# When the second half's tokens get their adaLN modulation: at the change of halves on ScalarE, or tile by tile ahead of it on VectorE

## The chip, the cores and the metric

The kernel runs on one core of one Trainium2 chip. The metric is the device time of one execution in microseconds. TensorE multiplies matrices; VectorE (DVE), ScalarE (ACT) and GpSimd (POOL) work on tiles in the on-chip memory; SyncE (SP) only issues transfers. The engines run on their own and wait for each other by semaphores.

## The reference

One layer of a decoder trunk over 2048 prompt tokens of width 1024, and 8 sample tokens. What matters here is how every projection's input comes about:

```python
ada = jax.nn.silu(c) @ w_ada + b_ada
shift, scale, gate = jnp.split(ada, 3, axis=-1)
hn = _rmsnorm(x, g_norm) * (1.0 + scale[:, None]) + shift[:, None]
z = hn @ w_in
xa, za, q, k, v, glr, zg = jnp.split(z, SPLITS, axis=-1)
# xa, za: conv, block-diagonal gates and a linear recurrence, gated by silu(za)
# q, k, v, glr, zg: 4 heads of gated linear attention, gated by silu(zg)
mix = jnp.concatenate([y_lru, y_gla], axis=-1) @ w_out
x = x + gate[:, None] * mix
```

The two groups' results go through one output projection, and a last RMSNorm follows. `scale` and `shift` are one number for each of the 1024 channels.

## The kernel before

The prompt is computed in two halves of 1024 tokens, first all projections, recurrence and attention of half 0, then those of half 1. For a half, `hn` lies transposed in SBUF, channels on the partitions: `hh` holds its values rounded to TensorE's 32-bit format and `hl` what the rounding left. Every projection is three matmuls for each slice of 128 channels, `acc<-hh,w`, `acc<-hl,w`, `acc<-hh,w` (L679 to L681; L364 to L366 for the values of the attention). Results are evicted from four accumulators, by ScalarE and VectorE: `vh` and `vl` (L975, L976) for values, `zs` (L1148, L1149) for gated columns.

Half 1's `hn` is prepared beside half 0's work. `turn_ahead(q)`, for q = 0 to 7, handles 128 tokens: SP loads `x` (L248); ScalarE squares it and sums (L166); VectorE makes the reciprocal root in twelve tiny operations (`rsqrt`, L148 to L154), scales the tile (`times`, L182) and transposes it in blocks of 32x32 (L253); SP stores it to DRAM (`xtd`, L257). The steps are put into a list by `after(units, fn)`, which counts units of TensorE's work, and are issued when their time has come: so their place in each engine's queue is fixed when the program is built, and an engine that comes to a step whose input is missing waits there with all that stands behind it.

At the change of halves `lru_last_a` projects the first group's last column block of half 0 and meanwhile fills `hh` and `hl` anew, in four groups g of 256 tokens. `hn_load` gathers the stored blocks (20 loads; twelve of them, `xst<-xtd` L277, stand together on SP). `modulate` takes scale (`Gm`) and shift (`Sh`) per channel on ScalarE (L201; a part of g = 3 on VectorE, L203) into `fs4` and `ra`, GpSimd rounds to `hh` (L204, 16 times), VectorE subtracts for `hl` (L205, 16 times). TensorE runs four gate projections of 256 tokens each there (`silu2`, evicted by `zs`). The steps of `modulate` are drawn one by one from the list `drips`. Behind them `sums` (L1508, L1512, L1517 on VectorE, L1511 on ScalarE) adds and subtracts the parts in `fs4` and `ra` to the operands `so` of seven products that stand for eight (L1576).

Other names in the prediction: `on` is an attention output chunk, normalized by L1108 and transposed by TensorE in L1182; `e`, `xb` and `g` belong to the decay of the attention (`decay` and `gla_decay`, L996 to L1045; TensorE takes `xb` in L1060); `tx`, `tg` and the scan (L1349 to L1353) are the recurrence; `cv`, `xh`, `xl` the conv and its rounding; `tr`, `th` prepare weights of pairs; `w<-wr` and `parts` prepare weights.

Of the kernel before, what the change touches and what calls it, by code (L numbers as in the profile page):

```python
# [54 lines left out]
def hybrid_kernel(ctx, tc, i, o):  # L55
    nc = tc.nc
    V, S, G, PE, SP = nc.vector, nc.scalar, nc.gpsimd, nc.tensor, nc.sync
# [117 lines left out]
    def scales(pool, ss, n, m=P):  # L175
        rs = pool.tile([P, 4], F32, tag="rs", name="rs", bufs=2)
        rsqrt(pool, rs[:m, :n], ss[:m, :n], n, m, 1.0 / D)
        return rs

    def times(xt, rs, m=P, j0=0):  # L180
        for j, x in enumerate(xt, j0):
            V.tensor_scalar(x[:m], x[:m], rs[:m, j:j + 1], None, op0=OP.mult)  # L182
# [2 lines left out]

        times(xt, scales(pool, squares(pool, xt, m, tag), len(xt), m), m)

    def modulate(xt, g, kts):

        c = slice(g * 256, (g + 1) * 256)  # L190
        pt = [x.rearrange("p (n k t) -> p k n t", k=KT, t=32) for x in xt]
        for k2 in range(kts[0], kts[1], 2):
            cg = slice(g % 2 * 256, g % 2 * 256 + 256)
            f = (fs4[(1, 2, 0)[k2 // 4 if g < 2 else 2]][:, k2 % 4:k2 % 4 + 2, cg] if g < 2 or k2 >= 4
                 else ra[k2 // 2][:, :, cg])
            for kt in range(k2, k2 + 2):
                for j, y in enumerate(pt):
                    n = 256 // len(pt)
                    z = f[:, kt - k2, j * n:(j + 1) * n].rearrange("p (n t) -> p n t", t=32)
                    if g < 3 or kt == k2:  # L200
                        S.activation(z, y[:, kt], AF.Identity, scale=Gm[:, kt, 8:9], bias=Sh[:, kt, 8:9])  # L201
                    else:
                        V.tensor_scalar(z, y[:, kt], Gm[:, kt, 8:9], Sh[:, kt, 8:9], op0=OP.mult, op1=OP.add)  # L203
            G.tensor_scalar(hh[:, k2:k2 + 2, c], f, 1.0, 0.0, op0=OP.mult, op1=OP.add)  # L204
            V.tensor_tensor(hl[:, k2:k2 + 2, c], f, hh[:, k2:k2 + 2, c].bitcast(F32), op=OP.subtract)  # L205

    def turn(xt, k):

# [36 lines left out]
    def turn_ahead(q):  # L245

        x, w = [xp.tile([P, TH + NS], F32, tag="xt", name="xt")[:, :D] for _ in range(2)]
        SP.dma_start(x, i["x_prompt"][0, TH + q * P:TH + (q + 1) * P])  # L248

        def scaled(ss):  # L250
            with behind(V):
                times([x], scales(xp, ss, 1))
                V.transpose(w.rearrange("p (c k j) -> p c k j", c=4, k=KT), x.rearrange("p (k c j) -> p c k j", c=4, k=KT))  # L253
# [7 lines left out]
        def squared():  # L261
            ss = squares(xp, [x])
            after(0.5, lambda: scaled(ss))

        after(2, squared)

    def hn_load(g):

        if g == 0:
            xt = [xp.tile([P, TH + NS], F32, tag="xt", name="xt")[:, :D] for _ in range(2)]  # L270
        else:
            xt = [xst[g - 1].rearrange("p q d -> p (q d)")]
        m = 2 // len(xt)
        for j, x in enumerate(xt):
            src = xtd[2 * g + j * m:2 * g + j * m + m].rearrange("q (a r) (c f) -> c r (q a) f", a=4, c=4)
            for c in range(4):
                SP.dma_start(x[32 * c:32 * c + 32].rearrange("r (n f) -> r n f", f=256), src[c])  # L277
        return xt

    fs = cp.tile([P, KT, NS], F32, name="fs")  # L280

# [457 lines left out]
    def ada_gate():  # L739

        pg = acc()

        def step(kt):
            ws = [xp.tile([P, TH + NS], F32, tag="xt", name="xt")[:, :D] for _ in range(2)]
            for n, w in enumerate(ws):
                SP.dma_start(w, i["w_ada"][0, (kt + n) * P:(kt + n + 1) * P, 2 * D:])

            def mm():
                for n in (1, 0):
                    for g in range(4):  # L750
# [12 lines left out]
        step(0)  # L763


    so, fs4, xst, ra, waiting = {}, [], [], [], ["gate", "pairs"]
    outw = {"stop": False, "next": None, "busy": False}

    def ready(what):
# [674 lines left out]
            for s in range(len(t.segs)):  # L1444
                za_unit(t, s)

    def next_hn(xt, g, k):

        modulate(xt[g], g, (k, k + 4))

    def lru_last_a(js):

        xa_load, xa_unit, za_load, za_unit = lru_units(0)
        xt = [hn_load(0)]
        lru(0, js[:-2])
        outw["stop"] = True
        lru(0, js[-2:-1])
        t = xa_load(js[-1])
        za_load(t)
        flush_gla()  # L1460
        while outw["busy"]:
            heapq.heappop(pend)[2]()
        open_sp()
        xt += [hn_load(1), hn_load(2), hn_load(3)]
        for s in range(2):
            xa_unit(t, s)
            za_unit(t, s)
            for g in range(2 * s, 2 * s + 2):
                for k in range(0, KT, 4):
                    drips.extend([lambda g=g, k=k: next_hn(xt, g, k), lambda: None])  # L1470

    spx = ExitStack()
    sp_ = None
# [1 line left out]
    def open_sp():  # L1475
        gpx.close()
        hpx.close()
        nonlocal sp_
        sp_ = spx.enter_context(tc.tile_pool(name="sp", bufs=1, side="right", reuse_waits="tile"))
        fs4[:] = [sp_.tile([P, 4, 512], F32, tag=f"s{n}", name="fs4") for n in range(2)]  # L1480
        xst[:] = [sp_.tile([P, 2, D], F32, tag=f"s{n}", name="xst") for n in range(3, 6)]
        fs4.append(sp_.tile([P, 4, 512], F32, tag="s2", name="fs4"))
        ra[:] = [new_ra(F32) for _ in range(2)]

# [17 lines left out]

    def sums():

        s1, s2, s4 = fs4

        def sub(x, y, z):
            V.tensor_tensor(x, y, z, op=OP.subtract)  # L1508

        def split(h, l, x):  # L1510
            S.copy(h, x)  # L1511
            V.tensor_tensor(l, x, h.bitcast(F32), op=OP.subtract)  # L1512

        def step(n, u):
            k = slice(2 * u, 2 * u + 2)
            if n == 0:
                V.tensor_tensor(s1[:, k], s1[:, k], ra[u], op=OP.add)  # L1517
                sub(ra[u], s2[:, k], ra[u])
                sub(s2[:, k], s1[:, k], s2[:, k])
            elif n == 3:  # L1520
                h, l = a21()
                split(h[:, k], l[:, k], ra[u])
            elif n == 4:
                if u == 0:
                    so[ZB22] = new_so(1), [new_ra(F32R) for _ in range(2)]
                h, l = so[ZB22]
                split(h[:, k], l[u], s4[:, k])
            else:
                if u == 0:
                    so[(ZT1, ZT2)[n - 1]] = [new_so(j) for j in ((3, 4), (5, 0))[n - 1]]  # L1530
                if n == 2:
                    sub(s4[:, k], s4[:, k], s2[:, k])
                h, l = so[(ZT1, ZT2)[n - 1]]
                split(h[:, k], l[:, k], (s1, s2)[n - 1][:, k])
# [741 lines left out]
```

## Time and profile before

| | us |
|---|---|
| median of 3 runs | 1459.3 (1457.58 to 1460.83) |
| the profiled execution | 1459.87 |
| its span | 1458.1 |
| TensorE busy in it | 1420.3 |
| VectorE, ScalarE, GpSimd busy | 1062.8, 692.9, 220.8 |

The mean granted clock is 0.992. In the timelines, a row gives start and duration in us, the engine, the line, the operation with output and inputs, the tile's shape, how many followed each other, and in brackets the idle time ahead of it and what ended it. Operations overlap a little on an engine, so the distance from start to start is shorter than the duration.

### The profile page before, as it was taken

What the parts mean: (1) busy time and instruction counts of PE and PEld (TensorE: products, weight loads), DVE (VectorE), ACT (ScalarE), POOL (GpSimd) and SP (SyncE); (2) the same over time, 40 slices, a digit from 0 to 9 for tenths busy, and PEclk for the clock granted to TensorE, in tenths of its full rate; (3) what the DMA queues carried; (4) which work ended last, traced back from release to release, by engine and by line L of the source; (5) the groups of instructions that cost most, each with busy time, mean ns of one, the idle gap of its engine ahead of it and who ended that gap; (6) DMA issues with size and microseconds to landing.
All of it is one profiled execution on the core that took longest, in us unless ns stands there. A gap on an engine that the chain in (4) does not pass through costs nothing.

```text
span 1458.1 us, 23543 instructions
## 1 busy us (share of the span) xinstructions
PE 1420.3 (97%) x8677; PEld 1249.5 (86%) x8677; DVE 1062.8 (73%) x2529; ACT 692.9 (48%) x1259; POOL 220.8 (15%) x366
## 2 busy tenths in 40 slices
PE   8999999989999999799999999999999999999998
PEld 6889988878888988688899999999998887778886
DVE  5757678966777578844548688686888986688886
ACT  3654544654365257623434454545567522144342
POOL 0200111121112113110110322423310000000000
PEclk9999999999999999899999999999999999999999
DMA  9755776875684558477754665665762767694453
GB/s 328 265 184 174 261 260 230 303 270 168 213 263 150 194 174 215 160 265 233 262 196 141 207 220 172 227 210 173 250 232 90 274 214 278 230 362 131 139 170 116
DMA packets 166424, 313.71 MB, mean 215 GB/s; under 512 B 13410, under 2 KB 94978, under 8 KB 163869
## 3 DMA queue, kind: packets, MB, share of 16 engines
q1 hardware_dynamic: 112405, 225.78, 45.8%
q0 software_dynamic: 22912, 70.96, 14.3%
q10 hardware_dynamic: 30992, 15.47, 3.6%
q8 instruction: 68, 1.11, 0.3%
q14 instruction: 47, 0.39, 0.1%
HBM read 192.70 MB, written 119.52 MB: 214 GB/s over the span
## 4 chain that ended last, share of the span: by engine, by line
PE 77%; issue 7%; DVE 7%; DMA 4%; ACT 4%; POOL 1%; DVEq 0%; SPq 0%; POOLq 0%; ACTq 0%
PE acc L1862 12%; PE acc L679 10%; PE acc L681 10%; PE acc L680 10%; PE tp L1862 9%; PE acc L1576 6%; PE acc L364 3%; PE acc L365 3%; PE acc L366 3%; PE po L1091 1%; DMA twd<-th 1%; PE acc L1334 1%; PE tp L1060 1%; PE tp L1182 1%; PE acc L1336 1%
## 5 line engine op out<-in xcount | busy, mean ns | idle before, releaser
L679 PE MATMUL acc<-hh,w 128*128 128x512 f32 (+3 forms) x1112 | 379.1, 341 | 6.5 <-DVE zs L1149 2.9
L680 PE MATMUL acc<-hl,w 128*128 128x512 f32 (+3 forms) x1112 | 376.5, 339 | 0.0
L681 PE MATMUL acc<-hh,w 128*128 128x512 f32 (+3 forms) x1112 | 376.5, 339 | 0.0
L679 PEld LDWEIGHTS acc<-hh,w 128*128 128x128 f32 x1112 | 210.8, 190 | 24.6 <-issue 4.1
L681 PEld LDWEIGHTS acc<-hh,w 128*128 128x128 f32 x1112 | 210.5, 189 | 16.5
L680 PEld LDWEIGHTS acc<-hl,w 128*128 128x128 f32 x1112 | 210.8, 190 | 15.2
L1862 PE MATMUL acc<-w,a 128*128 128x512 f32 (+1 forms) x792 | 184.9, 387 | 0.0
L1862 PEld LDWEIGHTS acc<-w,a 128*128 128x128 f32 x792 | 146.8, 188 | 33.2 <-issue 3.4
L364 PE MATMUL acc<-w,hh 128*128 128x256 f32 (+1 forms) x508 | 144.4, 284 | 1.6 <-DVE vl L976 0.8
L366 PE MATMUL acc<-w,hl 128*128 128x256 f32 (+1 forms) x508 | 142.9, 281 | 0.0
L365 PE MATMUL acc<-w,hh 128*128 128x256 f32 (+1 forms) x508 | 142.9, 281 | 0.0
L1862 PE MATMUL tp<-w,a 128*128 128x512 f32 x564 | 136.0, 391 | 0.0
L1862 PEld LDWEIGHTS tp<-w,a 128*128 128x128 f32 x564 | 105.2, 188 | 26.9 <-issue 5.2
L364 PEld LDWEIGHTS acc<-w,hh 128*128 128x128 f32 x508 | 95.7, 188 | 3.3 <-DVE vl L976 1.5
L366 PEld LDWEIGHTS acc<-w,hl 128*128 128x128 f32 x508 | 96.0, 189 | 0.0
L365 PEld LDWEIGHTS acc<-w,hh 128*128 128x128 f32 x508 | 95.8, 189 | 0.2
L1712 ACT CAST a<-s 128x512 fp32r<-128x512 f32 x61 | 36.5, 619 | 95.1 <-issue 35.6
L1148 ACT ACTIVATE zs<-acc 128x512 f32<-128x512 f32 (+3 forms) x70 | 34.2, 490 | 98.4 <-PE acc L681 95.3
L1297 DVE SCALAR_TENSOR_TENSOR cv<-xa,vecT,cv 128x512 f32<-128x512 f32 (+2 forms) x120 | 77.2, 646 | 3.6 <-ACT cv L1295 2.9
L1149 DVE SCALAR_TENSOR_TENSOR zs<-zs,acc 128x512 f32<-128x512 f32 (+3 forms) x70 | 38.5, 549 | 38.0 <-ACT zs L1148 38.0
L975 ACT CAST vh<-acc 128x256 fp32r<-128x256 f32 x56 | 20.5, 370 | 86.3 <-PE acc L366 69.8
L976 DVE TENSOR_TENSOR vl<-acc,vh 128x256 fp32r<-128x256 f32 x56 | 23.4, 420 | 48.5 <-ACT vh L975 48.5
(402 smaller groups left out, 2758.9 us busy)
## 6 DMA issues: line engine op xcount, KB each, us to landing
parts<-w SPq DMA_DIRECT2D x37, 1024.0 KB
w<-parts SPq DMA_DIRECT2D x28, 1024.0 KB
wr<-in_w_in_dram SPq DMA_DIRECT2D x38, 512.0 KB
a<-mixd SPq DMA_DIRECT2D x63, 256.0 KB
w<-wd SPq DMA_DIRECT2D x12, 1024.0 KB
w<-twd SPq DMA_DIRECT2D x20, 512.0 KB
wada<-in_w_ada_dram SPq DMA_DIRECT2D x16, 512.0 KB
mixd<-zs ACTq DMA_DIRECT2D x32, 256.0 KB
```

What stands on the lines that cost most here:

```text
L364: PE.matmul(ps, hh[:, kt, c], hi[:, kt % 4], start=kt == 0, stop=False)
L365: PE.matmul(ps, hh[:, kt, c], lo[:, kt % 4], start=False, stop=False)
L366: PE.matmul(ps, hl[:, kt, c], hi[:, kt % 4], start=False, stop=kt == KT - 1)
L679: PE.matmul(ps[:, :n], hi[:, kt], a, start=kt == 0, stop=False)
L680: PE.matmul(ps[:, :n], hi[:, kt], b, start=False, stop=False)
L681: PE.matmul(ps[:, :n], lo[:, kt], a, start=False, stop=kt == KT - 1)
L1148: S.activation(z, ps, AF.Tanh, scale=0.5)
L1149: V.scalar_tensor_tensor(z, z, 1.0, ps, op0=OP.add, op1=OP.mult)
L1297: V.scalar_tensor_tensor(cv[:, cq], xa[:, cq.start + k:cq.stop + k], cw[k], cv[:, cq], op0=OP.mult, op1=OP.add)
L1576: PE.matmul(ps, w[:, u, k], x[v][k], start=start and (k, u, v) == (0, 0, 0), stop=(k, u) == (3, 1), skip_group_check=True)
L1712: S.copy(t[:, 0, k], (low(t) if src is None else src)[:, k])
L1862: PE.matmul(ps, t[:, u, k], w[:, v, k, c], start=(q < 3 or ps is own) and (k, u, v) == (0, 0, 0), stop=(k, u) == (3, 1), skip_group_check= ...
```

## The change

The modulation of half 1's tokens moves into `turn_ahead`, between the transpose and the store. `spread_modulation` runs once ahead of tile 0: it brings scale and shift through DRAM (`gsd`, 2 stores, 8 loads) into a tile `gm` in which each value stands beside the 32 elements of a transposed block that need it. Each tile then gets a multiplication and an addition of 128x1024 with two operands (L284), its transpose is split in two, its Square is put one unit later, and it is stored in four pieces to `fd`, which lies as `fs4` and `ra` want it. `hn_load` becomes five loads: three contiguous ones of 1 MB into `fs4` and two into `ra` (L299 to L302). `modulate` only rounds and subtracts: 12 of the 16 roundings stay on GpSimd, 4 go to ScalarE (L206). The operands' inner order changes, so `sums` reads them through views of 32 elements (`blocked`, `natural`).

```diff
-    xtd = dpool.tile([8, P, D], F32, tag="xtd", name="xtd")
+    fd = dpool.tile([2, 2, P, 16, P], F32, tag="fd", name="fd")
+    gsd = dpool.tile([2, 2, P, 4], F32, tag="gsd", name="gsd")
...
-    def modulate(xt, g, kts):
+    def modulate(g, kts):
...
-            for kt in range(k2, k2 + 2):
-                for j, y in enumerate(pt):
-                    n = 256 // len(pt)
-                    z = f[:, kt - k2, j * n:(j + 1) * n].rearrange("p (n t) -> p n t", t=32)
-                    if g < 3 or kt == k2:
-                        S.activation(z, y[:, kt], AF.Identity, scale=Gm[:, kt, 8:9], bias=Sh[:, kt, 8:9])
-                    else:
-                        V.tensor_scalar(z, y[:, kt], Gm[:, kt, 8:9], Sh[:, kt, 8:9], op0=OP.mult, op1=OP.add)
-            G.tensor_scalar(hh[:, k2:k2 + 2, c], f, 1.0, 0.0, op0=OP.mult, op1=OP.add)
-            V.tensor_tensor(hl[:, k2:k2 + 2, c], f, hh[:, k2:k2 + 2, c].bitcast(F32), op=OP.subtract)
+            h, l = [natural(y[:, k2:k2 + 2, c]) for y in (hh, hl)]
+            if g > 1 and k2 % 4:
+                S.copy(h, f)
+            else:
+                G.tensor_scalar(h, f, 1.0, 0.0, op0=OP.mult, op1=OP.add)
+            V.tensor_tensor(l, f, h.bitcast(F32), op=OP.subtract)
...
+    def spread_modulation():
+
+        gw = cp.tile([P, KT, 32], F32, tag="sc", name="gw")
+        V.tensor_copy(gw[:, 0, :KT], Gm[:, :, 8])
+        V.tensor_copy(gw[:, 1, :KT], Sh[:, :, 8])
+        for n in range(2):
+            SP.dma_start(gsd[n].rearrange("h p k -> p h k"), gw[:, n, :KT].rearrange("p (h k) -> p h k", h=2))
+        gm = cp.tile([P, KT, 32], F32, tag="sc", name="gm")
+        for n in range(2):
+            for a in range(4):
+                SP.dma_start(gm[32 * a:32 * a + 32, n].rearrange("r (b k) -> r b k", k=4),
+                             gsd[n].rearrange("h (c r) k -> r (h c) k", c=4))
+        return gm
...
         def scaled(ss):
             with behind(V):
                 times([x], scales(xp, ss, 1))
-                V.transpose(w.rearrange("p (c k j) -> p c k j", c=4, k=KT), x.rearrange("p (k c j) -> p c k j", c=4, k=KT))
+                for h in range(2):
+                    y, z = [v[:, 512 * h:512 * h + 512] for v in (w, x)]
+                    V.transpose(y.rearrange("p (c k j) -> p c k j", c=4, k=4), z.rearrange("p (k c j) -> p c k j", c=4, k=4))
+            after(0.5, modulated)
+
+        def modulated():
+            w3 = w.rearrange("p (b j) -> p b j", j=32)
+            with behind(V):
+                for n, op in enumerate((OP.mult, OP.add)):
+                    V.tensor_tensor(w3, w3, gm[:, n, :, None].to_broadcast([P, 32, 32]), op=op)
             after(0.5, stored)
 
         def stored():
-            SP.dma_start(xtd[q], w)
+            for a in range(4):
+                SP.dma_start(fd[q // 4, :, :, 4 * (q % 4) + a].rearrange("h (c r) f -> r (h c) f", c=4),
+                             w[32 * a:32 * a + 32].rearrange("r (b f) -> r b f", b=8))
             if q < 7:
-                turn_ahead(q + 1)
...
+                turn_ahead(q + 1, gm)
+
+        after(3, squared)
...
-        after(2, squared)
...
+    def hn_load():
+
+        for n, x in ((0, fs4[1]), (1, fs4[2])):
+            SP.dma_start(x.rearrange("p k t -> p (k t)"), fd[0, n].rearrange("p n f -> p (n f)"))
+        for u in range(2):
+            SP.dma_start(ra[u].rearrange("p k t -> p (k t)").rearrange("p (n f) -> p n f", n=16), fd[1, 0][:, :, 64 * u:64 * u + 64])
+        SP.dma_start(fs4[0].rearrange("p k t -> p (k t)"), fd[1, 1].rearrange("p n f -> p (n f)"))
...
-                    turn_ahead(0)
+                    turn_ahead(0, spread_modulation())
...
-        xt = [hn_load(0)]
         lru(0, js[:-2])
...
-        xt += [hn_load(1), hn_load(2), hn_load(3)]
+        hn_load()
```

Where steps stand now, as the two programs' queues have it. First ScalarE at the decay of half 0's second head; before:

```order
L996 ACTIVATE e<-acc,vecT 128x512
L322 CAST w<-wr 128x1024
L998 ACT_TABLE_LOAD
L998 ACTIVATE e<-e 128x512
L166 ACTIVATE junk,ss<-xt 128x1024
L999 ACT_TABLE_LOAD
L999 ACTIVATE e<-e 128x512
```

and now:

```order
L1020 ACTIVATE e<-acc,vecT 128x512
L346 CAST w<-wr 128x1024
L1022 ACT_TABLE_LOAD
L1022 ACTIVATE e<-e 128x512
L1023 ACT_TABLE_LOAD
L1023 ACTIVATE e<-e 128x512
L1050 ACT_TABLE_LOAD
```

The Square of a tile of half 1 (`junk,ss<-xt`) no longer stands between the two steps of `e`. Next VectorE beside the eight value units of that head (`vl` is their eviction, one row for each; `tg`, `tx` the recurrence); before:

```order
L1350 SCALAR_TENSOR_TENSOR tg<-xl,tg 128x1024
L976 TENSOR_TENSOR vl<-acc,vh 128x256
L1351 TENSOR_TENSOR tx<-tx,tg 128x1024
L976 TENSOR_TENSOR vl<-acc,vh 128x256
L1353 SCALAR_TENSOR_TENSOR tg<-xl,tx 128x1024
L1392 TENSOR_TENSOR wg<-wgr,wg 128x256
```

and now:

```order
L1374 SCALAR_TENSOR_TENSOR tg<-xl,tg 128x1024
L819 TENSOR_TENSOR tr<-tr 128x512
L1375 TENSOR_TENSOR tx<-tx,tg 128x1024
L819 TENSOR_TENSOR tr<-tr 128x512
L1377 SCALAR_TENSOR_TENSOR tg<-xl,tx 128x1024
L284 TENSOR_TENSOR xt<-xt,gm 128x1024
L1380 COPY hc<-tg 128x1
L1395 SCALAR_TENSOR_TENSOR zs<-tg,zs 128x512
L284 TENSOR_TENSOR xt<-xt,gm 128x1024
L825 TENSOR_TENSOR tr<-tr,th 128x512 x2
L1000 TENSOR_TENSOR vl<-acc,vh 128x256
```

The second `vl`, which stood behind the product `tg`, stands behind the scan, both steps of a tile's modulation and four steps of `tr`. Last VectorE at the change of halves (fs_6007 and fs_6060 are `fs4[0]` of before and of the change, fs_6008 and fs_6061 `fs4[1]`); before:

```order
L205 TENSOR_TENSOR hl<-ra,hh 128x2x256 x2
L205 TENSOR_TENSOR hl<-fs_6007,hh 128x2x256 x2
L203 TENSOR_SCALAR ra<-xst,Gm,Sh 128x256 x2
L203 TENSOR_SCALAR fs_6007<-xst,Gm,Sh 128x256 x2
L205 TENSOR_TENSOR hl<-ra,hh 128x2x256 x2
L205 TENSOR_TENSOR hl<-fs_6007,hh 128x2x256 x2
L1517 TENSOR_TENSOR fs_6007<-fs_6007,ra 128x1024 x2
L1508 TENSOR_TENSOR ra<-fs_6008,ra 128x1024
L1512 TENSOR_TENSOR so<-fs_6007,so 128x1024
L1149 SCALAR_TENSOR_TENSOR zs<-zs,acc 128x256
```

and now:

```order
L209 TENSOR_TENSOR hl<-ra,hh 128x2x256
L1339 TENSOR_TENSOR xl<-cv,xh 128x512
L209 TENSOR_TENSOR hl<-fs_6060,hh 128x2x256 x2
L1173 SCALAR_TENSOR_TENSOR zs<-zs,acc 128x256
L1542 TENSOR_TENSOR fs_6060<-fs_6060,ra 128x2x16x32 x2
L1533 TENSOR_TENSOR ra<-fs_6061,ra 128x2x16x32
L1173 SCALAR_TENSOR_TENSOR zs<-zs,acc 128x256
L1533 TENSOR_TENSOR fs_6061<-fs_6060,fs_6061 128x2x16x32
L1537 TENSOR_TENSOR so<-fs_6060,so 128x1024
L1173 SCALAR_TENSOR_TENSOR zs<-zs,acc 128x256
```

The evictions `zs` of the gate projections stand between fewer sums: the first of these three stood ahead of the subtractions shown, and the third has one sum fewer ahead of it. On SP, the twelve `xst<-xtd` ahead of a `w<-parts` load become the three contiguous loads.

More of the change, by code (lines that the diff above doesn't have):

```diff
@@ L243, in apply_first, with turn_ahead, squared @@
         split(1)
-    def turn_ahead(q):
+    def spread_modulation():
[10 more added lines that the diff above has]
+        return gm
+    def turn_ahead(q, gm):
         x, w = [xp.tile([P, TH + NS], F32, tag="xt", name="xt")[:, :D] for _ in range(2)]
         SP.dma_start(x, i["x_prompt"][0, TH + q * P:TH + (q + 1) * P])
+        def squared():
+            ss = squares(xp, [x])
+            after(0.5, lambda: scaled(ss))
         def scaled(ss):
@@ L252, in scaled @@
                 times([x], scales(xp, ss, 1))
-                V.transpose(w.rearrange("p (c k j) -> p c k j", c=4, k=KT), x.rearrange("p (k c j) -> p c k j", c=4, k=KT))
+                for h in range(2):
[7 more added lines that the diff above has]
+                    V.tensor_tensor(w3, w3, gm[:, n, :, None].to_broadcast([P, 32, 32]), op=op)
             after(0.5, stored)
         def stored():
-            SP.dma_start(xtd[q], w)
+            for a in range(4):
+                SP.dma_start(fd[q // 4, :, :, 4 * (q % 4) + a].rearrange("h (c r) f -> r (h c) f", c=4),
+                             w[32 * a:32 * a + 32].rearrange("r (b f) -> r b f", b=8))
             if q < 7:
-                turn_ahead(q + 1)
-        def squared():
-            ss = squares(xp, [x])
-            after(0.5, lambda: scaled(ss))
-        after(2, squared)
[L267 to L278, printed above, removed]
+                turn_ahead(q + 1, gm)
[6 more added lines that the diff above has]
+        SP.dma_start(fs4[0].rearrange("p k t -> p (k t)"), fd[1, 1].rearrange("p n f -> p (n f)"))
     fs = cp.tile([P, KT, NS], F32, name="fs")
@@ L759, in mm @@
                     after(4, lambda: ready("gate"))
-                    turn_ahead(0)
+                    turn_ahead(0, spread_modulation())
             after(3, mm)
         step(0)
-    so, fs4, xst, ra, waiting = {}, [], [], [], ["gate", "pairs"]
+    so, fs4, ra, waiting = {}, [], [], ["gate", "pairs"]
     outw = {"stop": False, "next": None, "busy": False}
@@ L1445, in lru, with next_hn @@
                 za_unit(t, s)
-    def next_hn(xt, g, k):
-        modulate(xt[g], g, (k, k + 4))
+    def next_hn(g, k):
+        modulate(g, (k, k + 4))
     def lru_last_a(js):
         xa_load, xa_unit, za_load, za_unit = lru_units(0)
-        xt = [hn_load(0)]
         lru(0, js[:-2])
@@ L1480, in open_sp @@
         fs4[:] = [sp_.tile([P, 4, 512], F32, tag=f"s{n}", name="fs4") for n in range(2)]
-        xst[:] = [sp_.tile([P, 2, D], F32, tag=f"s{n}", name="xst") for n in range(3, 6)]
+        for n in range(3, 6):
+            sp_.tile([P, 2, D], F32, tag=f"s{n}", name="place")
         fs4.append(sp_.tile([P, 4, 512], F32, tag="s2", name="fs4"))
@@ L1503, in sums @@
     def sums():
-        s1, s2, s4 = fs4
+        s1, s2, s4 = [blocked(x) for x in fs4]
+        r = [blocked(x) for x in ra]
         def sub(x, y, z):
@@ L1516, in step @@
             if n == 0:
-                V.tensor_tensor(s1[:, k], s1[:, k], ra[u], op=OP.add)
-                sub(ra[u], s2[:, k], ra[u])
+                V.tensor_tensor(s1[:, k], s1[:, k], r[u], op=OP.add)
+                sub(r[u], s2[:, k], r[u])
                 sub(s2[:, k], s1[:, k], s2[:, k])
@@ L1521, in step @@
                 h, l = a21()
-                split(h[:, k], l[:, k], ra[u])
+                split(natural(h[:, k]), natural(l[:, k]), r[u])
             elif n == 4:
@@ L1526, in step @@
                 h, l = so[ZB22]
-                split(h[:, k], l[u], s4[:, k])
+                split(natural(h[:, k]), natural(l[u]), s4[:, k])
             else:
```

15 lines of the change are left out of this document (9 added, 6 removed).

## The prediction

> **What bounds the kernel now.** I read the page first, then the list of TensorE's waits, the windows around those waits, and the timelines of the engines in them.
>
> ```profile
> span 1458.1 us, 23543 instructions
> PE 1420.3 (97%) x8677; PEld 1249.5 (86%) x8677; DVE 1062.8 (73%) x2529; ACT 692.9 (48%) x1259; POOL 220.8 (15%) x366
> ```
>
> TensorE is busy for 97% of the span, so the change can gain only from the 38 us in which it stands still, and it can lose by adding to them. The list of waits says where they are (in total, times, longest):
>
> ```profile
> PE tp L1060 <- DVE xb L1045: 7.9, 2, 6.9
> PE acc L1334 <- DVE zs L1149: 3.8, 2, 2.5
> PE acc L679 <- DVE zs L1149: 2.9, 1, 2.9
> PE acc L679 <- DMA w<-parts: 2.8, 1, 2.8
> PE acc L364 <- DVE vl L976: 0.8, 1, 0.8
> ```
>
> Two places hold most of what this change can touch. One is the decay of the first half's linear attention (324 to 331 us, L1060); the other is the change of halves (584 to 604 us, the three rows behind it). The windows show how full VectorE is on the way there, and what a stall does afterwards (PE, PEld, DVE, ACT, POOL busy, then clock, DMA share, GB/s):
>
> ```profile
> 255.00:290.00 35.00, 35.00 (x197) 30.62 (x196) 31.92 (x71) 23.04 (x36) 6.71 (x11) 1.00 0.88 298
> 320.00:330.00 10.00, 3.88 (x17) 2.84 (x16) 4.29 (x12) 6.32 (x9) 0.00 (x0) 0.92 0.98 364
> 330.00:340.00 10.00, 9.19 (x40) 8.13 (x41) 8.18 (x21) 7.14 (x11) 0.87 (x2) 0.74 0.02 6
> 400.00:575.00 175.00, 175.00 (x957) 152.31 (x956) 122.06 (x234) 94.51 (x152) 33.77 (x57) 1.00 0.64 199
> 605.00:610.00 5.00, 5.00 (x17) 3.99 (x16) 5.00 (x6) 4.53 (x5) 0.00 (x0) 0.67 0.36 105
> ```
>
> In 255 to 290 VectorE is busy 91% of the time beside a TensorE that never stops; in 400 to 575 it is busy 70%. In 605 to 610, behind a stall of 2.86 us, the granted clock is 0.67: 5 x 0.33 = 1.7 us lost besides the stall itself, and a little before 605. I charge each stall over 2 us with about 1.8. [...]
>
> **Place 1: the decay at 324 us.** The rows are ACT's, VectorE's and TensorE's.
>
> ```profile
> 314.38 0.63 ACT L998 ACTIVATE e<-e 128x512 f32<-128x512 f32 x1
> 321.83 1.06 ACT L166 ACTIVATE junk<-xt 128x1024 bf16<-128x1024 f32 x1 [6.81 <-DMA xt<-in_x_prompt_dram]
> 324.29 0.63 ACT L999 ACTIVATE e<-e 128x512 f32<-128x512 f32 x1
> 328.87 0.69 DVE L1039 TENSOR_TENSOR e<-acc,e 128x512 f32<-128x512 f32 x1 [0.70 <-ACT e L1029]
> 323.49 0.39 PE L681 MATMUL acc<-hh,w 128*128 128x512 f32 x1
> 330.81 2.07 PE L1060 MATMUL tp<-xb,e 128*128 128x128 f32 x8 [6.94 <-DVE xb L1045]
> ```
>
> ACT stands 6.81 us at the Square of a second-half tile whose load hasn't landed, between the two halves of the decay's activation; the second half, VectorE's chain behind it and TensorE's transposes all come late. In the new order that Square is no longer between them. Then L999 comes straight behind L998's end at 315.0, with the 1.3 for its table that lie between the Square and 324.29: 316.3, 8.0 earlier, and e (L1039) is done at 321.5 instead of 329.5.
>
> Behind it, though, the new order puts the normalizing of the next tile ahead of g and xb. Its price is here (first and last of twelve tiny operations, then the scaling and the transpose):
>
> ```profile
> 308.31 0.14 DVE L148 TENSOR_SCALAR rs_x<-ss 128x1 f32<-128x1 f32 x1
> 310.61 0.75 DVE L182 TENSOR_SCALAR xt<-xt,rs 128x1024 f32<-128x1024 f32 x1
> 311.61 1.24 DVE L253 STREAM_TRANSPOSE xt<-xt 128x1024 f32<-128x1024 f32 x1
> ```
>
> From start to start that is 2.3 + 0.7 + 1.2, and with g and xb (0.6 each, 128x512 like L1039) xb is ready at 321.5 + 5.4 = 326.9. TensorE had nothing left at 323.7; the new order gives it nine more matmuls of 0.23 first, so it asks at 325.8: 1.1 us of stall stay, up to 3.4 if g's data from POOL's queue is late too. Removed: 6.94, and the slow clock of 330 to 340, 9.2 busy x 0.26 = 2.4. Net **-9.3 + 1.1 = -8.2**.
>
> **The new work on VectorE.** Each of eight tiles gets two multiplications or additions of 128x1024. The nearest row is L1508, of the same shape and kind with two operands in SBUF: 1.21, or 1.13 from start to start. 16 x 1.13 = 18.1 us. The last five tiles fall in 340 to 500, where VectorE has 30% left and TensorE waits for nothing: between 0 and 1.5 us, I take 0.5. The first three lie in the full stretch, and there they stand ahead of what TensorE waits for:
>
> ```profile
> 225.53 1.13 DVE L1108 TENSOR_SCALAR on<-on,ors 128x256 f32<-128x256 f32 x4
> 226.02 1.14 PE L1182 MATMUL tp<-ident,on 128*128 128x128 f32 x8 [0.33 <-DVE on L1108]
> 298.47 0.42 DVE L976 TENSOR_TENSOR vl<-acc,vh 128x256 fp32r<-128x256 f32 x1
> 298.80 1.22 DVE L1351 TENSOR_TENSOR tx<-tx,tg 128x1024 f32<-128x1024 f32 x1
> 302.66 2.28 DVE L1353 TENSOR_TENSOR_SCAN tg<-xl,tx 128x1024 f32<-128x1024 f32 x1
> 306.44 1.28 DVE L801 TENSOR_TENSOR tr<-tr,th 128x512 f32<-128x512 f32 x2
> 308.12 0.39 PE L364 MATMUL acc<-w,hh 128*128 128x256 f32 x1 [0.84 <-DVE vl L976]
> 310.97 0.39 PE L991 MATMUL acc<-gls,g2s 128*128 128x512 f32 x1
> ```
>
> (a) Already TensorE waits 0.33 for `on` at 226. The new order puts the first tile's scaling, transposes and modulation and four `tr` (128x512, 0.6) right ahead of it, 0.7 + 1.2 + 2.3 + 2.4 = 6.6, with some 0.3 where tiny operations of two norms alternate: `on` starts at 232.4 instead of 225.5. Its transposes on TensorE are moved back too, behind 37 matmuls of 0.12, to 230.1. Stall: 2 to 4, I take 2.5.
>
> (b) A column of value units at 287 to 311: one takes 2.85 (308.12 to 310.97), and the one at 308.12 waits for the `vl` four before it (ready 308.05). So the unit that starts at 308.12 - 0.84 - 2 x 2.85 = 301.6 needs the second `vl`, ready at 298.9 now. The new order puts it behind tx, the scan, the third tile's modulation, one zs and four tr. From the tg product, which waits for ACT as before (done at 298.5, or 297.4 as ACT has one cast fewer ahead of it): tx 1.1, two tr 1.2, scan 2.2, modulation 2.3, zs 0.6, two tr 1.2: 8.6, and 0.4 for itself: 306.4 to 307.5. Stall: 4.8. Both ends of this chain start from TensorE's own products, so the delay of (a) moves both and hides nothing here. It takes the place of the 0.84 and of 0.39 behind it.
>
> (c) The second tile's 2.3 delay the next gate's `xl`, but TensorE is late by then through (a): nothing.
>
> With slow clock after (a) and (b), 1.8 each: 2.5 + 4.8 + 3.6 - 1.2 = **+9.7**. Bounds: 4, if the queues shift so that (b) hides behind (a), and 14, if (c) counts too with its own slow clock.
>
> The two copies, two stores and eight loads that spread the modulation, and 24 more stores, are issues of 0.3 to 0.5 us on SP's queue. x's next load stands ahead of a tile's stores; the weight stores `parts<-w` and loads `wr` behind them wait up to 2 us longer for the modulation. Nothing in the list of waits names these: 0 to 1, taken as 0.
>
> **Place 2: the change of halves.** The first three rows are L205's group (least, median, longest in ns, first and last start), what it waited for (us, times), and L204's group; then the timelines of SP, ACT, VectorE and TensorE.
>
> ```profile
> L205 DVE TENSOR_TENSOR hl<-fs,hh x12: 676/680/1092, 572.4 to 594.9; 128x512 fp32r<-128x512 f32 x12
>   POOL hh L204: 2.3, 3
> L204 POOL TENSOR_SCALAR hh<-fs x12: 614/688/1717, 567.3 to 592.8; 128x512 fp32r<-128x512 f32 x12
> 558.66 21.92 SPq L277 DMA_DIRECT2D xst<-xtd  x12
> 565.60 4.35 ACT L201 ACTIVATE fs<-xt,Sh,Gm 128x128 f32<-128x128 f32 x11 [0.55 <-DMA wd<-p]
> 590.43 0.72 DVE L203 TENSOR_SCALAR ra<-xst,Gm,Sh 128x256 f32<-128x256 f32 x2
> 592.32 2.10 DVE L205 TENSOR_TENSOR hl<-ra,hh 128x512 fp32r<-128x512 f32 x2
> 595.55 2.35 DVE L1517 TENSOR_TENSOR fs<-fs,ra 128x1024 f32<-128x1024 f32 x2
> 597.82 1.21 DVE L1508 TENSOR_TENSOR ra<-fs,ra 128x1024 f32<-128x1024 f32 x1
> 603.82 0.41 DVE L1149 SCALAR_TENSOR_TENSOR zs<-zs,acc 128x256 f32<-128x256 f32 x1
> 604.38 0.77 PE L679 MATMUL acc<-hh,w 128*128 128x512 f32 x1 [2.86 <-DVE zs L1149]
> ```
>
> What decides is VectorE's chain: sixteen `hl` until 595.55, then seven sums, an eviction `zs` among them, and the eviction at 603.82, which frees the accumulator that TensorE takes at 604.38. The stall of 2.8 on w<-parts lies ahead of that and gives nothing by itself: its load stands behind twelve gathers on SP, which go, but TensorE then merely waits later.
>
> Removed from the chain: L203, 590.43 to 592.32, 1.9; VectorE's idle time behind POOL, 2.3 in three waits (POOL's roundings wait there for ACT's modulations, which go); and some of the time that roundings and subtractions take from each other (the pair at 592.32 took 2.10 beside POOL's last roundings, where two at the median take 1.36). Added: one conv and `xl` moved among the subtractions, with no net time. That the fs tiles are loaded only now costs nothing at first: their place comes free at 565.6 as for L201, 1 MB at 364 GB/s takes 2.9, so they land near 568.5, 571.4 and 574.3 and may be 3 us later than that: the first `hl` has its turn on VectorE at 572.4 as before, and the next ones are needed a subtraction and an eviction apart. The last `hl` ends at 595.55 - 1.9 - 2.3 = 591.3 if roundings stretch the subtractions as now, and at an estimated 588 if all sixteen take the median of L205's row; I take 590. Behind it stand three zs and six sums, 7.8, where before seven sums and two zs took 8.6: the accumulator is free at 597.8 instead of 604.2. TensorE could be there at 604.38 less 2.8, 2.5 and 2.9 of stalls and one slow clock, 594.4, so it still waits some 3 and pays the slow clock behind it as before. **-6.4**, between -4 (only the 1.9 and 2.3) and -10 (no wait left).
>
> **Sum.** -8.2 + 0.5 + 9.7 - 6.4 = -4.4 on the profiled execution, 1459.87, whose span is 1458.1; it lies 0.6 above the median of the runs, 1459.3. That is 1454.9 for the median, said as 1455.0. About 0.2%, 2.9 us, can be told from no change.
>
> **Rivals.** *The early additions cost more than both places give.* For it: VectorE is at 91% in 255 to 290, and each of three tiles adds 2.3 ahead of a result that TensorE takes within 3 us. If (c) counts (2.3 + 1.8) and the halves give only the lower end, -4: -8.2 + 0.5 + 13.8 - 4 = +2.1, and with the decay's rest stall at 3.4 (g late as well), +4.4: 1463.7. It decides once the early stalls exceed 14. Against it: (a) makes room for (c).
>
> *The early stalls are mostly covered*, because TensorE's lateness at (a) lets VectorE catch up before (b): 4 instead of 9.7, giving 1449.2. Against it: the chain at (b) starts at TensorE's own gate.
>
> *At the halves roundings and subtractions exclude each other.* With twelve roundings of 0.61 wholly in VectorE's way, `hl` ends at 588 + 7.3 = 595.3, as before; only the sum fewer ahead of the eviction is left, and -6.4 becomes -1: 1460.3, no change. [...] The trace agrees in part: that pair of subtractions took 0.74 longer, one rounding up to 1.72. Against the rival: half of the roundings would fall where VectorE is idle, or evicts, or has not come to the subtractions.
>
> **How the numbers follow.** Forecast 0.48, early loss 0.20, covered stalls 0.20, exclusion 0.12. Faster: the covered case and five sixths of the forecast's own spread, 0.60; same: the exclusion and the forecast's slow edge, 0.20; slower 0.20. Likeliest by itself 1450 to 1459. The range, 1446 to 1464, takes in the covered case with the halves' better end (-10: 1445.7) and the early loss.
>
> **What would show it.** Right: no L166 wait on x near 322 and no long L1060 wait; new TensorE waits of 2 to 5 us on `on` (L1132) near 230 and `vl` (L1000) near 305; the last `hl` (L209) ending 6 us earlier, against the end of the first half's last projection, than before, and with it the eviction at 604. Wrong: no wait at `vl` (then about 1449), or a first half later by over 4 us.

## The result and the profile after

The changed kernel takes 1452.6 us (median of 5 runs, 1449.6 to 1453.5); the kernel before took 1458.1 beside it (5 runs, 1457.5 to 1460.8). The ratio is 0.995, with a 95% interval of 0.994 to 0.997: faster by 0.5%. The profiled execution took 1452.74, its span is 1450.5. One execution of a later version, the one with eight roundings on ScalarE, took 4002.6 us; it counts as a slow run and is left out. From the page, and from the list of TensorE's waits (in total, times, longest):

```profile
span 1450.5 us, 23542 instructions
PE 1418.1 (98%) x8677; PEld 1246.9 (86%) x8677; DVE 1079.9 (74%) x2551; ACT 679.9 (47%) x1227; POOL 220.0 (15%) x362
```

```profile
PE acc L388 <- DVE vl L1000: 5.4, 1, 5.4
PE tp L1084 <- DVE xb L1069: 3.1, 2, 2.1
...
PE acc L703 <- DVE zs L1173: 1.9, 2, 1.7
PE acc L1358 <- DVE zs L1173: 1.7, 2, 1.4
...
PE acc L703 <- DMA w<-parts: 1.3, 1, 1.3
```

The 6.9 us for the decay's `xb` are gone (2.1 stay), the 2.8 for w<-parts at the change of halves too (the 1.3 for it now lie in half 1 and are new), and `vl` has become the longest wait of all. To see what each is worth, I set the start of every matmul in the new trace against that of the same matmul in the old one. The steps in that difference are the gains and losses in place, stall and slow clock together:

| place | foreseen | measured |
|---|---|---|
| (a) `on`, 230 us, with the old waits for `on` at 226 and 254 | +4.3 | -0.7 |
| (c) `xh` and `xl`, 279 us | 0 | +1.4 |
| (b) `vl`, 303 us, less the old waits for `vl` | +5.4 | +5.2 |
| place 1, the decay, 332 us | -8.2 | -5.3 |
| the last five tiles, 340 to 575 us | +0.5 | -0.4 |
| place 2, the change of halves | -6.4 | -7.5 |
| half 1 and the end | 0 | +0.6 |
| sum | -4.4 | -6.7 |

The two profiled executions also differ by 0.8 us ahead of 200 us, where the change does nothing yet; by the medians the change wins 5.6.

### The profile page after: what moved, and what is told of

The parts are those of the page before. It is cut to its first block, busy times and chain, and to the rows that moved or that the text cites. A ratio compares the mean times of both kernels' runs of the same rounds, so it can differ in the third digit from the quotient of the medians.

```text
span 1450.5 us, 23542 instructions
## 1 busy us (share of the span) xinstructions
PE 1418.1 (98%) x8677; PEld 1246.9 (86%) x8677; DVE 1079.9 (74%) x2551; ACT 679.9 (47%) x1227; POOL 220.0 (15%) x362
## 4 chain that ended last, share of the span: by engine, by line
PE 82%; DVE 9%; ACT 3%; DMA 3%; issue 2%; POOL 0%; DVEq 0%; SPq 0%; ACTq 0%
PE acc L1887 12%; PE acc L703 11%; PE acc L705 11%; PE acc L704 11%; PE tp L1887 9%; PE acc L1601 6%; PE acc L388 4%; PE acc L389 3%; PE acc L390 3%; PE po L1115 2%; DMA w<-parts 1%; DMA wada<-in_w_ada_dram 1%; PE acc L1358 1%; PE tp L1084 1%; PE tp L1206 1%
```

## The experiments

The expectations count in the changed kernel's lines; where a kernel has a line less or two, its rows differ by that. "The kernel before" was run again beside each group: 1459.3, 1460.0 and 1458.8. The changed kernel was run in the group with 1458.1 alone, so times of different groups compare to within 1 to 2 us.

**The decay alone.** The old kernel, with one tile's Square put off until it stands behind the decay; no modulation moves.

```diff
-        after(2, squared)
+        after(4.5 if q == 4 else 2, squared)
```

> The kernel before, with one number changed: the Square of the fifth tile of half 1 comes 4.5 units behind its load instead of 2, so that it and the normalizing behind it stand behind the decay on ScalarE and VectorE. Theory (the decay's stall is the Square's wait for its load): the wait of 6.9 on xb goes with its slow clock of 2.4: 1449 to 1450, and the change of halves stays as before. Rival (the chain on VectorE or the full DMA queues there bound the decay anyway): 1455 to 1458.

Measured: 1450.1 (1448.8 to 1452.8), ratio 0.994 (0.993 to 0.995). In ScalarE's timeline the second activation now follows the first directly, and in the list of waits `xb` is down from 7.9 to 1.0, which lies at another decay, in half 1:

```profile
313.43 0.63 ACT L998 ACTIVATE e<-e 128x512 f32<-128x512 f32 x1
...
315.38 0.63 ACT L999 ACTIVATE e<-e 128x512 f32<-128x512 f32 x1
```

```profile
PE tp L1060 <- DVE xb L1045: 1.0, 1, 1.0
```

One number in the old kernel is worth about as much as the whole change. By the matmuls' starts it gains 9.1 at the decay and 1.5 ahead of it, so the theory holds. What the change wins there comes from the Square's place, not from the modulation, and its own order gives 3.8 of the 9.1 back: it puts the normalizing of the next tile ahead of `xb`.

**No modulation.** The two operations L284 are left out, and half 1 gets neither scale nor shift.

```diff
-            with behind(V):
-                for n, op in enumerate((OP.mult, OP.add)):
-                    V.tensor_tensor(w3, w3, gm[:, n, :, None].to_broadcast([P, 32, 32]), op=op)
+            pass
```

> The changed kernel without the two operations per tile (half 1 gets neither scale nor shift); transposes, stores and loads stay. Theory (they cost through vl only): the wait of 5.4 and its slow clock of 1.7 go, the 1.2 of shorter waits behind come back, the 2.1 on xb stays: 5 to 7 faster than the changed kernel, 1446 to 1447.5. Rival (18 us on a full VectorE cost in more places than the list of waits names): over 8 faster.

Measured: 1448.9 (1446.5 to 1449.9), ratio 0.993 (0.991 to 0.994): 3.7 below the changed kernel where 5 to 7 were expected, and the longest wait is the same as with the modulation (a row of the waits; then ScalarE's and VectorE's timelines):

```profile
PE acc L386 <- DVE vl L998: 5.4, 1, 5.4
```

```profile
288.61 1.05 ACT L344 CAST w<-wr 128x1024 fp32r<-128x1024 f32 x1 [3.52 <-DMA wr<-in_w_in_dram]
289.57 0.68 ACT L1359 ACTIVATE tx<-acc,hbx 128x512 f32<-128x512 f32 x1
...
304.90 0.42 DVE L998 TENSOR_TENSOR vl<-acc,vh 128x256 fp32r<-128x256 f32 x1
```

The queues come out in another order without the two operations: ScalarE stands 3.52 us at a weight that hasn't landed, ahead of the evictions with which the recurrence begins, and `vl` still stands behind its scan. What the missing operations win was lost upstream, so the run can't price them at (b): `vl` is ready 1.6 earlier, and TensorE, which gains 1.4 at (c), asks for it about as much earlier. Another 1.5 come in half 1, where the wait for w<-parts stays out. The next run leaves the order nearly alone.

**The third tile's modulation shortened.**

```diff
-            w3 = w.rearrange("p (b j) -> p b j", j=32)
+            w3, m = w.rearrange("p (b j) -> p b j", j=32), 1 if q == 2 else 32
...
-                    V.tensor_tensor(w3, w3, gm[:, n, :, None].to_broadcast([P, 32, 32]), op=op)
+                    V.tensor_tensor(w3[:, :m], w3[:, :m], gm[:, n, :m, None].to_broadcast([P, m, 32]), op=op)
```

> The changed kernel, but the third tile's two modulating operations take 32 of the 1024 columns, so most of that tile of half 1 stays unmodulated; nothing else is changed, and all other queues but a few neighbours keep their order. In VectorE's queue the second vl then stands directly behind the scan and the first short operation. Theory (the wait for vl at 303 is this tile's modulation and what it pushes ahead of vl): scan from 300.2 to 302.4, vl ready by 303.1 where TensorE asks at 301.5, so 5.4 us of wait become 1.4 to 1.8, part of the slow clock (1.7) goes with it, and as the rest waits as before: 1447 to 1449. Rival (the scan and the third tile's earlier normalizing hold vl, as the run without any modulation, which had the same wait of 5.4, suggests): the wait falls by no more than 2 us: 1450 to 1452.

Measured: 1445.6 (1444.6 to 1446.8), ratio 0.991 (0.989 to 0.992). `vl` follows the scan, and the 5.4 became two waits of 1.2 and 1.1:

```profile
300.80 2.28 DVE L1377 TENSOR_TENSOR_SCAN tg<-xl,tx 128x1024 f32<-128x1024 f32 x1
303.00 0.16 DVE L284 TENSOR_TENSOR xt<-xt,gm 128x32 f32<-128x32 f32 x1
303.08 0.41 DVE L1000 TENSOR_TENSOR vl<-acc,vh 128x256 fp32r<-128x256 f32 x1
...
303.55 0.38 PE L388 MATMUL acc<-w,hh 128*128 128x256 f32 x1 [1.21 <-DVE vl L1000]
```

By the matmuls' starts it is 4.4 at this place: the theory holds, the wait is this tile's modulation and what it lets pass ahead of `vl`, one `zs` and two `tr`. A further 1.6 come at the halves, where the stall of 1.74 has no slow clock behind it (see the last section), and 1.6 in half 1, where the wait for w<-parts stays out. Nothing shows that these two come from the third tile; the 4.4 alone give 1448.2, inside the expected range.

**The modulation later.** First for all eight tiles, then for the first seven. With all eight, a part of the output is no longer the layer's (why is not settled here); the number of operations on each engine is that of the changed kernel.

```diff
-            after(0.5, modulated)
+            after(2, modulated)
```

> The changed kernel with each tile's modulation issued two units of work behind its transposes instead of half a unit. In the queue of VectorE the second vl then stands behind the tg product again, as before the change, and the next tile's normalizing stands behind xb. Theory (the early modulation costs through its place ahead of vl and, by its train, of xb): the waits of 5.4 on vl and 2.1 on xb go, with a slow clock of 1.7 behind each: 8 to 10 us faster than the changed kernel, about 1443. Rival (VectorE is simply full there, and the 18 us show up ahead of another result wherever they stand): 0 to 3 faster, 1450 to 1453, with new waits on on, xl or zs.

Measured: 1442.3 (1441.9 to 1443.7), ratio 0.989 (0.987 to 0.990), about what the theory said.

```diff
-            after(0.5, modulated)
+            after(2 if q < 7 else 0.5, modulated)
```

> The first seven tiles' modulation is put off by two units of TensorE's work instead of half a unit; the eighth tile stays as in the changed kernel. Theory (what counts is which results of TensorE's stand behind the tile's preparation in VectorE's queue, not the time that the modulation takes): in this order the second and third vl of the column at 303 stand ahead of the recurrence's scan again, and the normalizing stands behind the decay's xb. So the 5.4 us for vl with its slow clock (1.7) and 2 of the 3.1 us for xb with its slow clock (1.9) go: 1441.5 to 1444, as with all eight tiles (1442.3). Rival (with all eight tiles late, part of the gain came from the change of halves, where the last tile's stores stood elsewhere): 1 to 3 us come back, 1444 to 1446.

Measured: 1441.8 (1440.1 to 1442.8), ratio 0.988 (0.986 to 0.989). Its rows at (b) and its waits of 200 to 400 us, all of them:

```profile
300.64 0.42 DVE L1000 TENSOR_TENSOR vl<-acc,vh 128x256 fp32r<-128x256 f32 x1 [2.60 <-ACT vh L999]
300.98 2.28 DVE L1377 TENSOR_TENSOR_SCAN tg<-xl,tx 128x1024 f32<-128x1024 f32 x1
```

```profile
PE acc L703 <- DVE vl L1000: 1.1, 1, 1.1
PE acc L1359 <- DVE xl L1346: 0.9, 1, 0.9
```

`vl` stands ahead of the scan as in the old kernel, and VectorE waits for it instead of TensorE. All sixteen operations are still done, and at the decay, where the normalizing now stands behind `xb`, TensorE doesn't wait at all. By the matmuls' starts, against the changed kernel, 6.1 are won at (b) and 3.9 at the decay, and 1.5 are lost again from 345 to 500 us. Another 3.1 come later and are not this order's doing as far as the traces show: 1.6 at the halves, where the same stall has no slow clock behind it in this execution, and 1.5 in half 1, where the wait for w<-parts stays out. The theory holds for the two stalls that it names, and the rival (part of it came from the last tile's stores) falls.

**The whole preparation later.** The Square comes a unit later; the modulation stays right behind the transposes.

```diff
-        after(3, squared)
+        after(4 if q < 7 else 3, squared)
```

> The Square of the first seven tiles comes one unit later, and with it the whole preparation; the modulation still stands directly behind the transposes. Theory (the place in the queue): the second and third vl stand ahead of the scan and the normalizing behind xb, as where the modulation alone is late, so the same two stalls go: 1441.5 to 1445. Rival (the 2.3 us of the modulation themselves are what TensorE waits for, wherever they stand): one wait of 5 us is exchanged for waits of 2 to 4 us at the zs and xl behind which they now stand, near 270 to 285, each with its slow clock: 1446 to 1450.

Measured: 1448.0 (1447.1 to 1451.3), ratio 0.993 (0.991 to 0.994). No wait for `vl`, but between 270 and 345 us these:

```profile
PE tp L1084 <- DVE xb L1069: 1.7, 1, 1.7
PE acc L1358 <- ACT xh L1345: 1.2, 1, 1.2
PE acc L1359 <- DVE xl L1346: 0.6, 1, 0.6
```

Here the rival gave the number: against the run with seven tiles later, 4.9 us are lost between 195 and 335 us, most of it at `xh` and `xl` (2.7, a slow clock among it, 0.50 granted from 283 to 285); another 1.9 are lost at the halves, where the same stall of 1.7 has a slow clock behind it here and none there. Both theories hold in part. Moving the preparation frees `vl`, but the modulation next to its transposes then delays something else; two units behind them it found room.

**The roundings, all on GpSimd.**

```diff
-            if g > 1 and k2 % 4:
+            if False:
```

> The changed kernel with all 16 roundings at the change of halves on GpSimd (ScalarE's four go back). Theory (roundings and subtractions get in each other's way, and the last four roundings come one behind the other): the last hl ends 1.5 to 2.5 later, the eviction behind it too, and TensorE: 1454 to 1455. Rival (roundings are ahead of the subtractions anyway): no difference to the changed kernel, within 0.5.

Measured: 1451.8 (1450.6 to 1453.3), ratio 0.995 (0.994 to 0.996): no difference from the changed kernel. The number is the rival's, but the mechanism is the theory's: the last `hl` ends at 591.7 instead of 589.7, and the eviction that frees the accumulator starts at 598.0 instead of 596.0. TensorE still loses only 0.4. A new stall of 2.13 at 588.7, with a slow clock behind it (0.50 granted from 590 to 592), has made it 3.4 late by then, so at the eviction it waits 0.89 instead of 1.73, without the slow clock that the changed kernel has there. So this run can't price the roundings; the next runs ask the same from the other side.

**The roundings on ScalarE.** All sixteen, then eight, both on the kernel with seven tiles later.

```diff
-            if g > 1 and k2 % 4:
+            if True:
```

> As the run with seven tiles later, and all sixteen roundings at the change of halves are on ScalarE, none on GpSimd. Theory (GpSimd's roundings stretch VectorE's subtractions: 1.09 us each beside them, 0.68 alone): the first eight subtractions take 0.68 again, so the eviction that TensorE waits for at the halves (2.9 us, with slow clock behind it) comes some 3 us earlier: 2.5 to 4.5 us faster than the run with seven tiles later. Rival 1 (they are slow because of the inner order of 32 elements or the loads that land then): subtractions stay at 1.09, no difference within 1 us. Rival 2 (ScalarE's evictions zs stand behind four to six roundings of 0.6 and the wait for fs): 1 to 4 us slower.

Measured: 1437.8 (1436.9 to 1439.5), ratio 0.985 (0.984 to 0.986): 4.0 faster than the run with seven tiles later, as the theory had it.

```diff
-            if g > 1 and k2 % 4:
+            if k2 % 4:
```

> As the run with seven tiles later, and of the sixteen roundings eight are on ScalarE and eight on GpSimd (four and twelve in the changed kernel). Theory (GpSimd's roundings stretch VectorE's subtractions): half of the gain of sixteen on ScalarE, 1 to 2.5 us faster than the run with seven tiles later. Rival 1 (the stretching has another cause): no difference within 1 us. Rival 2 (ScalarE's evictions come late): 0.5 to 2 us slower.

Measured: 1440.2 (1439.8 to 1440.2, three runs), ratio 0.987 (0.985 to 0.988). The ratio of the run with seven tiles, 0.988, lies in this interval, so the times alone don't tell the two apart; by the matmuls' starts eight on ScalarE gain 1.6 at the halves, all sixteen 2.5. First the changed kernel, one subtraction beside a rounding in VectorE's timeline and the groups (busy time, mean ns); then the groups with sixteen on ScalarE, and the only wait that this kernel has from 560 to 640 us:

```profile
571.91 1.09 DVE L209 TENSOR_TENSOR hl<-fs,hh 128x512 fp32r<-128x512 f32 x1
```

```profile
L209 DVE TENSOR_TENSOR hl<-fs,hh 128x512 fp32r<-128x512 f32 x12 | 10.3, 885 | 0.0
L208 POOL TENSOR_SCALAR hh<-fs 128x512 fp32r<-128x512 f32 x10 | 9.5, 970 | 10.1 <-DMA fs<-fd 10.1
```

```profile
L209 DVE TENSOR_TENSOR hl<-fs,hh 128x512 fp32r<-128x512 f32 x12 | 7.9, 687 | 0.0
L206 ACT CAST hh<-fs 128x512 fp32r<-128x512 f32 x12 | 6.9, 623 | 5.1 <-DMA fs<-fd 5.1
```

```profile
PE acc L703 <- DVE zs L1173: 0.3, 1, 0.3
```

With GpSimd out of the way the twelve subtractions from `fs` take 0.69 each instead of 0.89 (it is 0.89 with seven tiles later too), and the eviction comes in time. The inner order of 32 elements and the loads are the same in both, so neither is the cause. This is the fastest version that was run, 1.5% below the old kernel and 1% below the changed one.

**The roundings on ScalarE and nothing else**, in the changed kernel (the same edit as for all sixteen above).

> The changed kernel with all sixteen roundings at the change of halves on ScalarE and nothing else changed. Theory (GpSimd's roundings beside VectorE's subtractions cost the change of halves 2.5 us whatever the first half does): subtractions 0.69 instead of 1.09 beside GpSimd, the wait of 1.7 for zs at the halves goes with its slow clock: 2.5 to 4 us faster than the changed kernel (1452.6), 1448.5 to 1450. Rival (the gain of ScalarE's roundings came from the later tiles' stores): within 1 us of it.

Measured: 1447.8 (1446.8 to 1449.5), ratio 0.993 (0.991 to 0.994), 4.8 below the changed kernel's median; 4.0 by the matmuls' starts at the halves, 1.5 more than on the kernel with seven tiles later, because the changed kernel has a slow clock there and that one has none. GpSimd's roundings cost the change of halves whatever the first half does, 4.0 here and 2.5 there. The old kernel with both its Square later and its roundings on ScalarE was not run, so how much of the 1437.8 needs the moved modulation stays open.

## Why the prediction came out right

The forecast of 1455.0 and its range hold the result. The picture is the forecast's: gains at both places, a part of them given back by VectorE's new work, some 45% where I had 70%. But (a) missed by 5.0, place 1 by 2.9, and (c) and place 2 by 1.4 and 1.1; that these nearly cancel is luck. The early stalls (a) to (c) come to 5.9, nearer to the 4 of the covered case than to my 9.7, though not by that rival's mechanism: no lateness at (a) covered (b), which came in full.

**(a) The wait for `on` did not come.** The step that failed is "`on` starts at 232.4". I added 6.9 us to `on`'s old start, 225.5, for the first tile's scaling, transposes and modulation and four `tr`. Of these only the modulation, 2.3, is new ahead of `on`. In the old kernel the scaling, the transposes and the four `tr` stood ahead of it too, only earlier, ahead of the tiny operations that make `on`'s factor (`rs_x<-oss` is the first of them):

```profile
214.25 0.76 DVE L182 TENSOR_SCALAR xt<-xt,rs 128x1024 f32<-128x1024 f32 x1
...
217.67 0.69 DVE L795 TENSOR_TENSOR tr<-tr 128x512 f32<-128x512 f32 x1
...
221.64 0.15 DVE L148 TENSOR_SCALAR rs_x<-oss 128x4 f32<-128x4 f32 x1
```

In the changed kernel they stand among these tiny operations, the first of which starts at 218.68:

```profile
221.72 0.75 DVE L183 TENSOR_SCALAR xt<-xt,rs 128x1024 f32<-128x1024 f32 x1
222.50 1.30 DVE L277 STREAM_TRANSPOSE xt<-xt 128x512 f32<-128x512 f32 x2
...
227.93 1.22 DVE L284 TENSOR_TENSOR xt<-xt,gm 128x1024 f32<-128x1024 f32 x1
229.07 1.13 DVE L1132 TENSOR_SCALAR on<-on,ors 128x256 f32<-128x256 f32 x4
...
229.56 1.14 PE L1206 MATMUL tp<-ident,on 128*128 128x128 f32 x8
```

From that first operation to `on` it takes 10.4 where it took 3.9, and these 6.5 more are about what I charged. But the way begins 3.0 earlier, because what moved into it no longer stands ahead of it. `on` starts at 229.07, 3.3 before my figure, and TensorE takes it 0.5 later without a wait. The 2.5 and the slow clock were charged for nothing.

**(b) came as foreseen**, 5.4 of stall for 4.8, by the chain that was worked out (recurrence, scan, modulation, `zs`, `tr`, `vl`):

```profile
296.68 1.22 DVE L1374 SCALAR_TENSOR_TENSOR tg<-xl,tg 128x1024 f32<-128x1024 f32 x1
...
300.16 2.28 DVE L1377 TENSOR_TENSOR_SCAN tg<-xl,tx 128x1024 f32<-128x1024 f32 x1
...
306.48 0.41 DVE L1000 TENSOR_TENSOR vl<-acc,vh 128x256 fp32r<-128x256 f32 x1
...
306.95 0.58 PE L388 MATMUL acc<-w,hh 128*128 128x256 f32 x1 [5.42 <-DVE vl L1000]
```

The short third tile shows the reason: with it the wait is 1.2. **(c)** was put at nothing because TensorE would be late by (a). It wasn't, and (c) cost 1.4, two short stalls with what they delay:

```profile
278.27 0.73 PE L1358 MATMUL acc<-xh,wg 128*128 128x512 f32 x2 [0.44 <-ACT xh L1345]
...
280.09 0.50 PE L1359 MATMUL acc<-xl,wg 128*128 128x512 f32 x1 [0.39 <-DVE xl L1346]
```

Without the modulation both stalls are gone, and so are the 1.4.

**Place 1.** The Square is gone from between the two activations, as foreseen. The rest stall was mis-sized: 2.14 instead of 1.1, and I gave it no slow clock, which it had. Most of the missing 1.0 lies ahead of the chain that I summed up: the first activation starts 5.8 later than in the old trace (320.18 against 314.38), TensorE's work only 5.1.

```profile
332.21 0.68 DVE L1069 SCALAR_TENSOR_TENSOR xb<-acc,xb 128x512 f32<-128x512 f32 x1
...
332.94 1.16 PE L1084 MATMUL tp<-xb,e 128*128 128x128 f32 x8 [2.14 <-DVE xb L1069]
335.05 0.63 PE L703 MATMUL acc<-hh,w 128*128 128x512 f32 x1
```

```profile
335.00:340.00 5.00, 5.00 (x21) 4.09 (x20) 4.96 (x14) 3.29 (x5) 0.00 (x0) 0.75 0.02 3
```

The granted clock of 0.75 over these 5 us is 1.3 us more. In the run with seven tiles later the normalizing stands behind `xb`, and the wait isn't there.

**Place 2** was right in mechanism and nearly in size. The last `hl` ends at 589.7 (foreseen 590), and the eviction that frees the accumulator at 596.4; TensorE waits 1.73 for it where I had 3:

```profile
588.46 1.28 DVE L209 TENSOR_TENSOR hl<-fs,hh 128x512 fp32r<-128x512 f32 x2
...
596.00 0.41 DVE L1173 SCALAR_TENSOR_TENSOR zs<-zs,acc 128x256 f32<-128x256 f32 x1
...
596.56 0.47 PE L703 MATMUL acc<-hh,w 128*128 128x512 f32 x1 [1.73 <-DVE zs L1173]
597.64 0.63 PE L703 MATMUL acc<-hh,w 128*128 128x512 f32 x1
```

The rival of mutual exclusion did not decide, since the gain held, but roundings and subtractions do get in each other's way: moved to ScalarE, the roundings give back another 2.5 to 4. The rows say a stretch: 1.09 for 0.69 in the subtraction, and 0.97 for GpSimd's rounding where the best in the old trace took 0.61 (the profile's spans on GpSimd are rough). That one of the two wholly shuts out the other, as the rival had it, no run shows; whether the stretch is a block for part of the time the trace can't tell.

## What to carry to other kernels

Work that is free on a busy engine in total is not free where a result that the bottleneck takes stands behind it (5.4 us of stall at `vl` here): ask which of TensorE's operands follow the new instructions in that queue, and put a gap between a chain's steps if they do not have to be neighbours. But a place in a queue is not a time: before charging all that stands ahead of a result, look which of it stood ahead of that result before, only earlier in the queue, and charge what is new. And where one engine rounds and another subtracts, try the rounding on an engine that doesn't stretch the subtraction (here 0.69 with all sixteen on ScalarE, 0.89 with twelve of them on GpSimd).

## What the runs showed of the hardware

The same stall is followed by a slow clock in one execution and not in another. The stall of 1.7 us for `zs` at the halves left matmuls of 0.63 behind it in the changed kernel (above) and of 0.40 in the run with seven tiles later; the 2.14 for `xb` left 0.63 in the changed kernel and 0.40 with all sixteen roundings on ScalarE and nothing else, though the roundings lie 240 us further on. The granted clock is 0.62 from 596 to 600 against 1.00 from 588 to 593 in the first pair, and 0.75 against 1.00 from 335 to 340 in the second. First the run with seven tiles later, then that one:

```profile
588.33 0.47 PE L703 MATMUL acc<-hh,w 128*128 128x512 f32 x1 [1.72 <-DVE zs L1173]
589.79 0.40 PE L703 MATMUL acc<-hh,w 128*128 128x512 f32 x1
```

```profile
335.03 1.16 PE L1084 MATMUL tp<-xb,e 128*128 128x128 f32 x8 [2.14 <-DVE xb L1069]
336.70 0.40 PE L703 MATMUL acc<-hh,w 128*128 128x512 f32 x1
```

Between 100 and 1420 us of the twelve traces, eleven of the twelve stalls of 2.3 us and more have slow matmuls behind them; behind the twelfth, 2.47 for `zs` in the old kernel, only three matmuls run, of 0.39 to 0.50, and then the next stall stands, with 0.50 granted in it from 602 to 604. Of those under 1.7 only one has, 1.2 with another of 0.6 right behind it; of the twelve between 1.7 and 2.2 seven have. What decides whether the clock drops no run shows, and my charge of 1.8 for each stall over 2 us was an estimate from the one row behind 2.86. For a forecast the counts mean that a stall near 2 us has two prices, 1.6 us apart by the matmuls' starts in both pairs above, and that two versions which differ by that much may differ in nothing else.
